# Down projection of a diffusion layer: inner partial sums kept in PSUM, a new order of the seven inner products, and last residual rows written into PSUM ahead of the products

## The chip, the core and the metric

The kernel runs on one core of a Trainium2 chip. The time is the device time of one launch in microseconds (us), the median of several runs. The engines are TensorE (PE, with its weight loads as PEld), VectorE (DVE), ScalarE (ACT), GpSimd (POOL) and SyncE (SP), which issues the transfers here.

## The reference

One layer of a diffusion backbone with 2048 positions and a width of 1024: a token mixer, then a SwiGLU block, each with a residual and a layer norm behind it. The change touches only the last product, `@ wd`, with the sum and the norm around it:

```python
def swiglu(u, wg, wu, wd):
    return (jax.nn.silu(u @ wg) * (u @ wu)) @ wd
...
        u2 = modulate(layer_norm(x), sh2, sc2)
        x = layer_norm(DEEPNORM_ALPHA * x + gt2 * swiglu(u2, w_ffn_gate[l], w_ffn_up[l], w_ffn_down[l]),
                       ln2_g[l], ln2_b[l])
```

The hidden width is 2816, so this product is (2048 x 2816) by (2816 x 1024). The gate `gt2` is multiplied into the weights beforehand.

## The kernel before

All products here are made from two fp16 parts (a high one and the rest), three matmuls for each, by `mm3` (L152 to L154). The down projection takes about the last 437 us (1757 to 2194), and is a Strassen-Winograd scheme of two levels.

**The outer level** has seven operands: A11, A12, S2, S3, A22, S1, S4. The hidden activations (float32 for the first five, `h_d`) and the weights (`wd_d`) of each lie in DRAM, written by earlier stages. The results go into 16 tiles of SBUF named `state`, one for each half `sb` of the rows, each half f of such a half, and each of the names "a", "11", "21" and "22", [128, 2, 512] in float32. A11 begins "a"; A12 plus "a" is "11", which is one quadrant of the output; S2 is added to "a"; S3 plus "a" is "21", which is copied to "22"; A22 is added to "21". S1 and S4 complete "22" and "a".

**The inner level** applies to the first five outer operands. For each o of these and each `sb`, in this text a *step* (A11/0, A11/1, A12/0, and so on, ten in all), the hidden block is cut into four quadrants `h0` to `h3`, loaded by `h_load` into one buffer each in the order 0, 2, 3, 1. `h_ops` makes the seven inner operands out of them. Names A11 to S4 stand for these too; the index into the tuple is the product:

```python
                if i == 1:
                    G.tensor_tensor(s1, q[2], q[3], ALU.add)
                    V.tensor_tensor(q[2], q[0], q[2], ALU.subtract)
                    V.tensor_tensor(q[0], s1, q[0], ALU.subtract)
                elif i == 2:
                    G.tensor_tensor(q[1], q[1], q[0], ALU.subtract)
                t = op((q[0], q[1], q[0], q[2], q[3], s1, q[1])[i])
```

So A11 is `h0` and A12 is `h1`. Then POOL makes `s` (tile `s1`, h2 + h3, L1394), VectorE makes S3 in the place of `h2` (L1395) and S2 in the place of `h0` (L1396), and POOL makes S4 in the place of `h1` (L1398). A22 is `h3` itself and S1 is `s`. Each operand is split into a tile `ho` by `half_split`: ScalarE casts the high part (L1134), VectorE subtracts it for the low part (L1135). There are three buffers of `ho`. The seven products of a step run in the order A11, A12, S2, S3, A22, S1, S4; each has 30 matmuls of [128 x 128] by [128 x 256], and four of them have 6 more ("ride", for the 22nd hidden block, with its own small operand in a tile named `raw`), 234 in all. Each product takes the next one of the eight PSUM banks in turn (`proj`, `misc`, `tq`, `zt`, `s0`, `s1`; the trace prints the last two as `s`, as it does the SBUF tile).

Behind each product, results are read out of its bank: ScalarE copies A11 to an SBUF tile `p` (L1500); VectorE adds A12 to `p` into a tile `c`, S2 onto `p`, S3 to `p` into `b`, A22 to `b` into `c`, S1 onto `p`, and `p` or `b` to a bank into `c` for the rest (L1504 to L1511, and L1443 in `outer`). `outer` then adds `c` to a state (L1445 to L1452), SBUF to SBUF. When a half f of a step is complete, `block_done` adds residual rows for A12 (to "11"), S3 (to "a" and "22") and A22 (to "21"), by one VectorE instruction over 1024 columns each (L1411), with the rows loaded into a `raw` tile (three buffers). For A12 and A22 `moments` follows, with statistics for the norm (L1419).

**The last two outer operands**, S1 and S4 (`ONE`), run without an inner level, as products 512 wide over four banks; `after` adds a bank to its states and ends the norm (`finish`).

The order of instructions on each engine is that of a list scheduler that simulates the program when it is built; the blocks under `tc.high_priority()` go ahead of others. SP's queue issues all loads of these steps in that order; `issue_after(before)` holds the loads of a step behind the last `h` load of the step before. A load of `h` waits until its buffer's last reader in the step before is done. With a step of sb 0, SP also loads the seven weight tiles of that operand (`w_load`, L1207).

Of the kernel before, what the change touches and what calls it, by code (L numbers as in the profile page):

```python
# [11 lines left out]
AF = mybir.ActivationFunctionType  # L12
# [67 lines left out]
def layer_kernel(ctx: ExitStack, tc: tile.TileContext, a, out):  # L80
# [19 lines left out]
    def mk(pool, shape, dt=F32, tag=None, bufs=1):  # L100
        return pool.tile(shape, dt, name=nm(tag), tag=tag, bufs=bufs)
# [26 lines left out]
    def raw_tile(shape=(P, 2, 512), dt=F32):  # L128
        return mk(wp, list(shape), dt, tag="raw", bufs=3)
# [809 lines left out]

    A11, A12, S2, S3, A22, S1, S4 = range(7)  # L940
    ORDER = (A11, A12, S2, S1, S3, A22, S4)

    def left(q, s, eng):

# [425 lines left out]
    def state(name, sb, f):  # L1370

        key = (name, sb, f)
        if key not in ST:
            ST[key] = mk(dq, [P, 2, 512], tag="state", bufs=16)
        return ST[key]

    def h_ops(q, last):

        lt = raw_tile((P, 2, 768), F16)
        with tc.high_priority():  # L1380
            half_split(lt[:, :, 0:512], last)
            G.tensor_tensor(last[:, 0:256], last[:, 0:256], last[:, 256:512], ALU.subtract)
            half_split(lt[:, :, 512:768], last[:, 0:256])

        def op(src):
            t = mk(d1, [P, 2, HP, 256], F16, tag="ho", bufs=3)
            half_split(t, src)
            return t

        s1 = mk(d1, [P, HP, 256], tag="s1")  # L1390
        for i in range(7):
            with tc.high_priority():
                if i == 1:
                    G.tensor_tensor(s1, q[2], q[3], ALU.add)  # L1394
# [5 lines that stand above are left out]
            yield t, lt  # L1400
# [1 line left out]

    RIDE = {1: (0, 0), 4: (1, 0), 5: (1, 1), 6: (2, 1)}

    def residual(sb, f, name, row, hf):
        s_ = state(name, sb, f)
        xr = raw_tile((P, 2, 512))
        for i in range(2):
            t = sb * 8 + row * 4 + f * 2 + i
            Q.dma_start(xr[:, i], x1_d[t][:, hf * 512 : hf * 512 + 512])  # L1410
        V.scalar_tensor_tensor(s_, xr, ALPHA * RS, s_, ALU.mult, ALU.add)  # L1411

    st6 = {}

# [15 lines left out]
            V.tensor_tensor(r, r, b2[:, fs], ALU.add)  # L1430
            Q.dma_start(outv[t * P : (t + 1) * P, fs], r)

    def outer(o, sb, f, y, src, ps):


        def st(name):
            return state(name, sb, f)[:, :, y * 256 : (y + 1) * 256]

        if o == A11:
            V.tensor_tensor(st("a"), src, ps, ALU.add)  # L1440
            return
        c = mk(dq, [P, 2, 256], tag="c", bufs=2)
        V.tensor_tensor(c, src, ps, ALU.add)  # L1443
        if o == A12:
            V.tensor_tensor(st("11"), st("a"), c, ALU.add)  # L1445
        elif o == S2:
            V.tensor_tensor(st("a"), st("a"), c, ALU.add)
        elif o == S3:
            V.tensor_tensor(st("21"), st("a"), c, ALU.add)
            S.copy(st("22"), st("21"))  # L1450
        else:
            V.tensor_tensor(st("21"), st("21"), c, ALU.add)  # L1452

    def block_done(o, sb, f):

        if o == A12:
            residual(sb, f, "11", 0, 0)
            for i in range(2):
                moments(sb, f, i, "11", 0, 0)
        elif o == S3:  # L1460
            residual(sb, f, "a", 0, 1)
            residual(sb, f, "22", 1, 1)
        elif o == A22:
            residual(sb, f, "21", 1, 0)
            for i in range(2):
                moments(sb, f, i, "21", 0, 1)

    for o in range(5):
        for sb in range(2):
            if o == 0 and sb == 0:  # L1470
                w = w_next
                hq, last, before = h_next
                w.update((q, w_load(0, q)) for q in (5, 6))
            else:

                with tc.issue_after(before):
                    if sb == 0:
                        w = {0: w_load(o, 0)}
                    hq, last, before = h_load(o, sb)
                    if sb == 0:  # L1480
                        wl = wl_load(o)
                        w.update((q, w_load(o, q)) for q in range(1, 7))
            if o == 0 and sb == 1:
                g2 = rows(dq, a["ln2_g"], "row0")
                b2 = rows(dq, a["ln2_b"], "row1")
            p = b_ = None
            for q, (h, lt) in enumerate(h_ops(hq, last)):
                ps = bank(ALL_BANKS, (P, 2, 256))
                ride = RIDE.get(q)
                for i in range(2):  # L1490
                    ts_ = slice(i * P, (i + 1) * P)
                    for k in range(HP):
                        mm3(ps[:, i], h[:, 0, k, ts_], h[:, 1, k, ts_], w[q][k][:, :, 0], w[q][k][:, :, 1], k == 0, k == HP - 1 and ride is None)
                    if ride:
                        r0 = ride[0] * 256 + i * P
                        ys = slice(ride[1] * 256, ride[1] * 256 + 256)
                        mm3(ps[:, i], lt[:, 0, r0 : r0 + P], lt[:, 1, r0 : r0 + P], wl[:, 0, ys], wl[:, 1, ys], False, True)
                if q == 0:
                    p = mk(dq, [P, 2, 256], tag="p", bufs=2)
                    S.copy(p, ps)  # L1500
                elif q == 1:
                    outer(o, sb, 0, 0, p, ps)
                elif q == 2:
                    V.tensor_tensor(p, p, ps, ALU.add)  # L1504
                elif q == 3:
                    b_ = mk(dq, [P, 2, 256], tag="b", bufs=1)
                    V.tensor_tensor(b_, p, ps, ALU.add)
                elif q == 4:
                    outer(o, sb, 1, 0, b_, ps)
                elif q == 5:  # L1510
                    V.tensor_tensor(p, p, ps, ALU.add)  # L1511
                    outer(o, sb, 1, 1, b_, ps)
                    block_done(o, sb, 1)
                else:
                    outer(o, sb, 0, 1, p, ps)
                    block_done(o, sb, 0)


    slots = [(tag, 1) for tag in ("h0", "h2", "h3", "s1", "h1")] + [("ho", 3)] * 3
# [28 lines left out]
    for o in ONE:  # L1548
        w = one_w(o)
        for sb in range(2):  # L1550
            h = one_h(o, sb)
            pts = [bank(ALL_BANKS) for _ in range(4)]

            def product(j, it):
                ts_ = slice(it * P, (it + 1) * P)
                mm3(pts[it], h[j][:, 0, ts_], h[j][:, 1, ts_], w[j][:, :, 0], w[j][:, :, 1], j == 0, j == HJ - 1)

            def after(it):
                f, i = divmod(it, 2)
                pv = pts[it].rearrange("p (c y n) -> p y c n", c=2, y=2)  # L1560

                def add(name):
                    r = state(name, sb, f)[:, i].rearrange("p (y c n) -> p y c n", c=2, y=2)
# [50 lines left out]
```

## Time and profile before

| | |
|---|---|
| median of three runs | 2194.33 us (2192.77 to 2195.07) |
| the profiled execution | 2195.93 us, span 2194.1 us |
| TensorE (PE) busy | 2051.6 us, 94% of the span |
| VectorE (DVE) busy | 1487.7 us, 68% |
| GpSimd (POOL) busy | 845.6 us, 39% |
| ScalarE (ACT) busy | 803.5 us, 37% |
| mean granted TensorE clock | 0.973 of full speed |

The shares are means over the whole program; the change concerns 1757 us to the end. TensorE is close to always busy, so what is to be read is where it waits in that part and for what.

### The profile page before, as it was taken

To read this page: it belongs to the slowest core of one execution; us is meant where nothing else is said; L and a number is where in the kernel's file an instruction comes from. 1 tells how busy PE (TensorE), PEld (TensorE's weight loads), DVE (VectorE), ACT (ScalarE), POOL (GpSimd) and SP (SyncE) were. 2 spreads that over 40 slices of the span, in tenths; PEclk is the share of its full clock that TensorE was granted. 3 is DMA by queue.
4 is the path that set the end of the run, shared out by engine and by line. 5 is a ranking of instruction groups with operands and counts; after the bars stand their busy time and mean duration, and the time that the engine had idled before them with its cause. 6 is when DMAs were issued, how large, how long until landed. Compare 5 with 4: busy or idle time off the path is not lost. (4 is left out here: it accounts for less than half of the span.)

```text
span 2194.1 us, 31196 instructions
## 1 busy us (share of the span) xinstructions
PE 2051.6 (94%) x11678; PEld 1185.6 (54%) x11678; DVE 1487.7 (68%) x2731; ACT 803.5 (37%) x1442; POOL 845.6 (39%) x838
## 2 busy tenths in 40 slices
PE   6987999999999999889999999999999979898997
PEld 4545676567558444434444444444443458776743
DVE  7767584765688677876656665666556278878866
ACT  5634542332223244443343333333433233333222
POOL 3412321221221156656556655665565142222110
PEclk8998999999999999989999999999999989999999
DMA  9502321221142566614343334343434186779543
GB/s 285 175 4 77 106 80 49 78 61 47 55 119 90 194 209 218 207 66 154 126 144 133 118 129 150 126 136 130 139 116 156 55 266 189 214 213 278 200 146 128
DMA packets 308745, 305.20 MB, mean 139 GB/s; under 512 B 14753, under 2 KB 248049, under 8 KB 307441
## 3 DMA queue, kind: packets, MB, share of 16 engines
q1 hardware_dynamic: 301776, 287.08, 40.9%
q10 hardware_dynamic: 6816, 16.12, 2.0%
q8 instruction: 92, 1.51, 0.3%
q14 instruction: 61, 0.49, 0.1%
HBM read 200.25 MB, written 102.90 MB: 138 GB/s over the span
## 5 line engine op out<-in xcount | busy, mean ns | idle before, releaser
L152 PE MATMUL proj<-ws,uhi 128*128 128x512 f16 (+1 forms) x768 | 251.1, 327 | 2.1 <-ACT sg L751 1.0
L154 PE MATMUL proj<-ws,ulo 128*128 128x512 f16 (+1 forms) x768 | 250.8, 327 | 0.0
L153 PE MATMUL proj<-ws,uhi 128*128 128x512 f16 (+1 forms) x768 | 250.7, 326 | 0.0
L153 PEld LDWEIGHTS <-ws 128*128 128x128 f16 x1296 | 128.2, 99 | 175.9 <-issue 26.6
L152 PEld LDWEIGHTS <-ws 128*128 128x128 f16 x1296 | 128.4, 99 | 157.1 <-issue 9.4
L154 PEld LDWEIGHTS <-ws 128*128 128x128 f16 x1296 | 128.0, 99 | 156.4 <-issue 6.7
L149 DVE SCALAR_TENSOR_TENSOR ws<-raw,ws 128x512 f16<-128x512 f32 x186 | 156.1, 855 | 75.3 <-ACT ws L148 74.3
L148 ACT ACTIVATE ws<-raw 128x512 f16<-128x512 f32 x186 | 112.4, 624 | 124.3 <-DMA raw<-in_w_ffn_gate_dram 36.6
L152 PE MATMUL proj<-u2b,ws 128*128 128x512 f16 x340 | 128.8, 383 | 10.3 <-ACT b L1294 6.3
L152 PE MATMUL misc<-u2a,ws 128*128 128x512 f16 x344 | 131.6, 382 | 6.0 <-ACT p L1294 3.8
L153 PE MATMUL misc<-u2a,ws 128*128 128x512 f16 x344 | 131.8, 383 | 0.0
L154 PE MATMUL misc<-u2a,ws 128*128 128x512 f16 x344 | 131.7, 383 | 0.0
L154 PE MATMUL proj<-u2b,ws 128*128 128x512 f16 x340 | 130.2, 383 | 0.0
L153 PE MATMUL proj<-u2b,ws 128*128 128x512 f16 x340 | 130.1, 383 | 0.0
L1134 ACT CAST ho<-h 128x1280 f16<-128x1280 f32 x60 | 75.0, 1258 | 126.3 <-DMA h<-h 29.0
L149 DVE SCALAR_TENSOR_TENSOR wdo<-raw,wdo 128x256 f16<-128x256 f32 (+1 forms) x100 | 63.4, 655 | 84.8 <-ACT wdo L148 83.8
L167 POOL TENSOR_TENSOR rstd<-ve,mhalf 128x1 f32<-128x1 f32 x66 | 38.4, 590 | 200.8 <-DVE ve L165 177.9
L207 DVE SCALAR_TENSOR_TENSOR macc<-raw,sil,macc 128x128 f32<-128x128 f32 x308 | 109.2, 387 | 3.2
L1135 DVE TENSOR_TENSOR ho<-h,ho 128x1280 f16<-128x1280 f32 x60 | 104.2, 1743 | 9.7 <-ACT ho L1134 9.7
L149 DVE SCALAR_TENSOR_TENSOR wdo<-ws,wdo 128x512 f16<-128x512 f32 (+2 forms) x70 | 59.3, 868 | 75.8 <-ACT wdo L148 74.3
L154 PEld LDWEIGHTS <-ho 128*128 128x128 f16 x764 | 76.2, 100 | 51.1 <-DVE ho L1135 34.2
L152 PEld LDWEIGHTS <-uhi 128*128 128x128 f16 x768 | 75.8, 99 | 44.0 <-issue 2.5
(496 smaller groups left out, 5498.6 us busy)
## 6 DMA issues: line engine op xcount, KB each, us to landing
h<-h SPq DMA_DIRECT2D x40, 640.0 KB, 5.4
raw<-in_w_mod_dram SPq DMA_DIRECT2D x44, 512.0 KB, 4.1
wd<-wdo SPq DMA_DIRECT2D x50, 448.0 KB, 2.5
wd<-wd SPq DMA_DIRECT2D x33, 640.0 KB, 8.5
h<-sg SPq DMA_DIRECT2D x66, 256.0 KB, 2.6
raw<-in_w_ffn_gate_dram SPq DMA_DIRECT2D x22, 512.0 KB, 4.7
raw<-in_w_ffn_up_dram SPq DMA_DIRECT2D x22, 512.0 KB, 5.8
h<-hs SPq DMA_DIRECT2D x44, 256.0 KB, 2.0
```

The lines of the kernel that those rows point to most:

```text
L148: S.activation(hi, raw, AF.Copy, scale=scale)
L149: V.scalar_tensor_tensor(lo, raw, scale, hi, ALU.mult, ALU.subtract)
L152: T.matmul(o, sh, mh, start=first, stop=False, skip_group_check=onto)
L153: T.matmul(o, sh, ml, start=False, stop=False, skip_group_check=onto)
L154: T.matmul(o, sl, mh, start=False, stop=last, skip_group_check=onto)
L167: pows.append(G.tensor_tensor(rstd, ve, mhalf[:, 0:n], ALU.pow).ins)
L207: V.scalar_tensor_tensor(acc, raw[:, k], sil[:, v, k : k + 1], acc, ALU.mult, ALU.add)
L1134: S.copy(dst[:, 0], src)
L1135: V.tensor_tensor(dst[:, 1], src, dst[:, 0], ALU.subtract)
```

## The change

Each step now lets its products accumulate in PSUM. The order of products is `DOWN`: A11, A12, S2, S1, S3, S4, A22. Three banks serve a step: one (`x`) for A11, S2, S3 and A22 on top of each other, one for A12, and one (`z`) for S1 and S4. Between two products on a bank it is read out: after A11, A12, S2, S1, S3, S4 and A22, the last seen sum goes from the bank to a state at once, in one VectorE instruction by the table `INTO` (for the first A11 of a state a copy by ScalarE). The tiles `p`, `b` and `c` are gone. "22" is no longer copied from "21": its residual instruction reads "21" and writes "22". The residual rows of the states "a" are no longer added in step S3; in the outer S4 stage ScalarE writes them, scaled, into the four banks before the first matmul, and the matmuls accumulate onto them (`onto`).

```diff
+    DOWN = (A11, A12, S2, S1, S3, S4, A22)
...
-        for i in range(7):
+        for i in DOWN:
...
+    def x1_half(t, hf):
+        return x1_d[t][:, hf * 512 : hf * 512 + 512]
+
+    def residual(sb, f, name, row, hf, onto=None):
+
         xr = raw_tile((P, 2, 512))
         for i in range(2):
-            t = sb * 8 + row * 4 + f * 2 + i
-            Q.dma_start(xr[:, i], x1_d[t][:, hf * 512 : hf * 512 + 512])
-        V.scalar_tensor_tensor(s_, xr, ALPHA * RS, s_, ALU.mult, ALU.add)
+            Q.dma_start(xr[:, i], x1_half(sb * 8 + row * 4 + f * 2 + i, hf))
+        V.scalar_tensor_tensor(state(name, sb, f), xr, ALPHA * RS, state(onto or name, sb, f), ALU.mult, ALU.add)
...
-    def outer(o, sb, f, y, src, ps):
-
+
+    INTO = {A11: ("a", None), A12: ("11", "a"), S2: ("a", "a"), S3: ("21", "a"), A22: ("21", "21")}
+    begun = set()
+
+    def outer(o, sb, f, y, ps):
+
+        into, of = INTO[o]
+        if (o, sb, f, y) in begun:
+            of = into
+        begun.add((o, sb, f, y))
...
-        if o == A11:
-            V.tensor_tensor(st("a"), src, ps, ALU.add)
-            return
-        c = mk(dq, [P, 2, 256], tag="c", bufs=2)
-        V.tensor_tensor(c, src, ps, ALU.add)
...
-            V.tensor_tensor(st("21"), st("a"), c, ALU.add)
-            S.copy(st("22"), st("21"))
+        if of is None:
+            S.copy(st(into), ps)
         else:
-            V.tensor_tensor(st("21"), st("21"), c, ALU.add)
+            V.tensor_tensor(st(into), st(of), ps, ALU.add)
...
-            residual(sb, f, "a", 0, 1)
-            residual(sb, f, "22", 1, 1)
+            residual(sb, f, "22", 1, 1, "21")
...
+            x = z = None
+            for q, (h, lt) in zip(DOWN, h_ops(hq, last)):
+                onto = x if q in (S2, S3, A22) else z if q == S4 else None
+                ps = bank(ALL_BANKS, (P, 2, 256)) if onto is None else onto
...
+                        mm3(
+                            ps[:, i], h[:, 0, k, ts_], h[:, 1, k, ts_], w[q][k][:, :, 0], w[q][k][:, :, 1],
+                            onto is None and i == 0 and k == 0, k == HP - 1 and ride is None, skip,
+                        )
...
+                if q == A11:
+                    x = ps
+                    outer(o, sb, 0, 0, x)
+                elif q == A12:
+                    outer(o, sb, 0, 0, ps)
+                elif q == S2:
+                    outer(o, sb, 0, 1, x)
+                elif q == S1:
+                    z = ps
+                    outer(o, sb, 1, 1, z)
+                elif q == S3:
+                    outer(o, sb, 1, 1, x)
+                elif q == S4:
+                    outer(o, sb, 0, 1, z)
+                    block_done(o, sb, 0)
+                else:
+                    outer(o, sb, 1, 0, x)
                     block_done(o, sb, 1)
...
+            onto = o == S4
+            if onto:
+                for it in range(4):
+                    xr = raw_tile((P, 512))
+                    Q.dma_start(xr, x1_half(sb * 8 + it, 1))
+                    S.activation(pvs[it], xr.rearrange("p (y c n) -> p y c n", c=2, y=2), AF.Copy, scale=ALPHA * RS)
```

On ScalarE, these rows are the casts of the seven operands of step A12/0 into `ho`, and what else stands among them; the tile read stands behind the arrow, so `h0` to `h3` are the quadrants and `s1` the sum. Before:

```order
L1134 CAST ho_2864_16814<-h0_2850_16783 128x1280
L1134 CAST ho_2867_16853<-h1_2853_16789 128x1280
L1134 CAST ho_2871_16898<-h0_2850_16783 128x1280
L1134 CAST ho_2873_16933<-h2_2851_16785 128x1280
L1500 COPY p_2866_16848<-tq_2865_16817 128x512
L1134 CAST ho_2876_16969<-h3_2852_16787 128x1280
L1134 CAST ho_2880_17013<-s1_2863_16813 128x1280
L1134 CAST ho_2886_17065<-h1_2853_16789 128x1280
```

Of the change (its lines stand one or a few further down):

```order
L1135 CAST ho_2852_16800<-h0_2838_16769 128x1280
L1135 CAST ho_2855_16839<-h1_2841_16775 128x1280
L1451 COPY state_2833_16651<-s1_2826_16499 128x2x256
L1135 CAST ho_2857_16881<-h0_2838_16769 128x1280
L1135 CAST ho_2858_16915<-s1_2851_16799 128x1280
L1135 CAST ho_2861_16957<-h2_2839_16771 128x1280
L1135 CAST ho_2862_16991<-h1_2841_16775 128x1280
L1135 CAST ho_2866_17039<-h3_2840_16773 128x1280
```

The cast of `h3` moved from fifth of the seven to last, that of the sum from sixth to fourth.

On SP, these rows are the loads of step A12/1 (`h` quadrants, then the block for the small operand, `ws`, and its weights). Before:

```order
L1216 DMA h0_2892_17116<-h_1956_9749 128x5x256
L1216 DMA h2_2893_17118<-h_1956_9749 128x5x256
L1216 DMA h3_2894_17120<-h_1956_9749 128x5x256
L1216 DMA h1_2895_17122<-h_1956_9749 128x5x256
L1218 DMA ws_2932_17445<-h_1944_9743 128x512
L1223 DMA ws_2933_17447<-wl_1986_9764 128x1024
```

Of the change:

```order
L1217 DMA h0_2870_17087<-h_1956_9749 128x5x256
L1217 DMA h2_2871_17089<-h_1956_9749 128x5x256
L1217 DMA h1_2873_17093<-h_1956_9749 128x5x256
L1219 DMA ws_2900_17401<-h_1944_9743 128x512
L1224 DMA ws_2901_17403<-wl_1986_9764 128x1024
L1217 DMA h3_2872_17091<-h_1956_9749 128x5x256
```

The load of `h3` moved from the third place to the last, behind `h1` and the two `ws` tiles.

On VectorE, these rows are the boundary from A12/0 to A12/1: the splits of the new step (`ho` from `h`), the two sums that make its operands (L1395 and L1396 before, L1396 and L1397 now), and what is left of the old step. Before:

```order
L1135 TENSOR_TENSOR ho_2899_17133<-h0_2892_17116,ho_2899_17133 128x1280
L1396 TENSOR_TENSOR h0_2892_17116<-s1_2898_17132,h0_2892_17116 128x1280
L1511 TENSOR_TENSOR p_2866_16848<-p_2866_16848,s1_2881_17016 128x512
L1443 TENSOR_TENSOR c_2882_17054<-b_2875_16967,s1_2881_17016 128x512
L1135 TENSOR_TENSOR ho_2902_17172<-h1_2895_17122,ho_2902_17172 128x1280
L1445 TENSOR_TENSOR state_2879_17011<-state_2817_16397,c_2882_17054 128x2x256
L1443 TENSOR_TENSOR c_2888_17105<-p_2866_16848,proj_2887_17068 128x512
L1411 SCALAR_TENSOR_TENSOR state_2879_17011<-raw_2883_17057,state_2879_17011 128x1024
L1445 TENSOR_TENSOR state_2870_16895<-state_2809_16283,c_2888_17105 128x2x256
L1135 TENSOR_TENSOR ho_2906_17217<-h0_2892_17116,ho_2906_17217 128x1280
```

Of the change:

```order
L1136 TENSOR_TENSOR ho_2880_17143<-h1_2873_17093,ho_2880_17143 128x1280
L1396 TENSOR_TENSOR h2_2871_17089<-h0_2870_17087,h2_2871_17089 128x1280
L1422 BN_STATS st6_2864_17035<-state_2854_16834 128x6
L1422 BN_STATS st6_2865_17037<-state_2854_16834 128x6
L1136 TENSOR_TENSOR raw_2875_17097<-ws_2874_17095,raw_2875_17097 128x512
L1453 TENSOR_TENSOR state_2860_16955<-state_2812_16359,tq_2853_16803 128x2x256
L1397 TENSOR_TENSOR h0_2870_17087<-s1_2876_17103,h0_2870_17087 128x1280
L1453 TENSOR_TENSOR state_2879_17138<-state_2827_16530,misc_2878_17107 128x2x256
L1414 SCALAR_TENSOR_TENSOR state_2860_16955<-raw_2867_17079,state_2860_16955 128x1024
L1136 TENSOR_TENSOR raw_2875_17097<-ws_2874_17095,raw_2875_17097 128x256
L1136 TENSOR_TENSOR ho_2882_17185<-h0_2870_17087,ho_2882_17185 128x1280
```

The two operand sums stand behind the split of A12 and among statistics and a read-out of the old step now; the sum in the place of `h0` (L1396 before, L1397 now) stood ahead of the split of A12 and now stands behind it. No row adds an SBUF tile `c` to a state any more.

## Rows read from the trace of the kernel before

**Rows 1.** Windows: start and end (us), length, busy time (instructions) by engine, clock, DMA.
```profile
core 0: us, PE busy (x) PEld busy (x) DVE busy (x) ACT busy (x) POOL busy (x), PEclk, DMA share, GB/s
1757.00:1831.00 74.00, 60.07 (x484) 49.12 (x483) 58.38 (x46) 24.20 (x27) 29.32 (x12) 0.91 0.89 270
1831.00:1856.50 25.50, 25.50 (x236) 22.78 (x235) 21.18 (x19) 9.29 (x8) 5.80 (x2) 1.00 0.54 171
1856.50:1887.40 30.90, 27.20 (x237) 23.56 (x235) 24.96 (x28) 8.96 (x9) 6.85 (x3) 0.94 0.73 220
1887.40:1918.70 31.30, 26.16 (x237) 22.57 (x235) 31.30 (x32) 12.92 (x14) 8.89 (x4) 1.00 0.54 158
1918.70:1946.40 27.70, 25.88 (x237) 22.72 (x234) 20.93 (x21) 8.28 (x8) 7.24 (x3) 1.00 0.77 223
1946.40:1975.90 29.50, 26.06 (x236) 22.65 (x234) 24.78 (x23) 11.69 (x11) 6.12 (x2) 1.00 0.63 188
1975.90:2007.20 31.30, 27.04 (x236) 23.41 (x234) 28.91 (x26) 11.24 (x13) 7.44 (x3) 0.95 0.81 240
2007.20:2040.80 33.60, 27.75 (x236) 23.32 (x235) 30.07 (x28) 12.29 (x13) 8.74 (x3) 0.95 0.87 283
2040.80:2070.10 29.30, 27.38 (x244) 23.41 (x241) 28.05 (x31) 7.64 (x8) 5.14 (x2) 1.00 0.70 249
2070.10:2127.00 56.90, 56.90 (x267) 25.86 (x265) 26.24 (x53) 5.97 (x8) 2.94 (x4) 1.00 0.47 145
```

**Rows 2.** Waits, 1831 to 2070: group, releaser, idle us, count, longest.
```profile
PEld L154 <- DVE ho L1135: 25.7, 13, 4.5
```

**Rows 3.** Timeline of PE in A12/1: start, duration, wait and releaser in brackets.
```profile
1865.69 0.39 PE L154 MATMUL zt<-wd,ho 128*128 128x256 f16 x1 [3.69 <-DVE ho L1135]
```

**Rows 4.** Timeline of DVE, 1856.9 to 1868.7.
```profile
1859.70 0.68 DVE L1443 TENSOR_TENSOR c<-p,proj 128x512 f32<-128x512 f32 x1
1860.30 3.33 DVE L1411 SCALAR_TENSOR_TENSOR state<-raw,state 128x1024 f32<-128x1024 f32 x1
1864.15 1.48 DVE L1135 TENSOR_TENSOR ho<-h,ho 128x1280 f16<-128x1280 f32 x1
...
1867.35 1.20 DVE L1411 SCALAR_TENSOR_TENSOR state<-raw,state 128x1024 f32<-128x1024 f32 x1
```

**Rows 5.** Timeline of POOL in the same stretch.
```profile
1859.31 3.23 POOL L1398 TENSOR_TENSOR h<-h,h 128x1280 f32<-128x1280 f32 x1 [8.51 <-DVE ho L1135]
```

**Rows 6.** The chain of waits: first at 1840 to 1850, then at 1873 to 1892.
```profile
1842.44 5.30 DMA h<-h
1847.91 2.91 POOL s L1394
...
1875.46 8.28 DMA h<-h
```

**Rows 7.** One window behind the wait of rows 3; columns as in rows 1.
```profile
1865.40:1868.80 3.40, 3.11 (x15) 2.24 (x16) 3.40 (x6) 0.41 (x1) 0.73 (x1) 0.50 0.83 259
```

**Rows 8.** Groups of ScalarE, 1757 to 2195: count, busy, mean ns, idle before.
```profile
L1134 ACT CAST ho<-h 128x1280 f16<-128x1280 f32 x60 | 75.0, 1258 | 126.3 <-DMA h<-h 29.0 <-PE misc L154 23.6 <-PE s L154 21.3
L1500 ACT COPY p<-proj 128x512 f32<-128x512 f32 x3 | 1.7, 578 | 0.0
```

**Rows 9.** DMA issues, 1757 to 2066: count, size, median us to landing.
```profile
h<-h SPq DMA_DIRECT2D x36, 640.0 KB, 4.7
wd<-wd SPq DMA_DIRECT2D x31, 640.0 KB, 8.5
```

**Rows 10.** Groups of VectorE by form, 1757 to 2075; columns as in rows 8.
```profile
L1395 DVE TENSOR_TENSOR h<-h,h 128x1280 f32<-128x1280 f32 x10 | 14.9, 1486 | 20.3 <-POOL s L1394 20.3
L1419 DVE BATCH_NORM_STATS2 st<-state 128x6 f32<-128x512 f32 x16 | 10.2, 678 | 0.1
```

**Rows 11.** Timeline of SP at 1783: a weight load of the first step.
```profile
1782.99 3.66 SPq L1207 DMA_DIRECT2D wd<-wd  x2
```

**Rows 12.** Timeline of PE: last matmul of the fifth product, then of the eighth.
```profile
1789.80 0.27 PE L154 MATMUL proj<-ws,raw 128*128 128x256 f16 x1
...
1808.56 0.27 PE L154 MATMUL zt<-wd,ho 128*128 128x256 f16 x1
```

More of the change, by code (lines that the diff above doesn't have):

```diff
@@ L1403, in layer_kernel @@
     RIDE = {1: (0, 0), 4: (1, 0), 5: (1, 1), 6: (2, 1)}
-    def residual(sb, f, name, row, hf):
-        s_ = state(name, sb, f)
+    def x1_half(t, hf):
+        return x1_d[t][:, hf * 512 : hf * 512 + 512]
+    def residual(sb, f, name, row, hf, onto=None):
         xr = raw_tile((P, 2, 512))
         for i in range(2):
-            t = sb * 8 + row * 4 + f * 2 + i
-            Q.dma_start(xr[:, i], x1_d[t][:, hf * 512 : hf * 512 + 512])
-        V.scalar_tensor_tensor(s_, xr, ALPHA * RS, s_, ALU.mult, ALU.add)
+            Q.dma_start(xr[:, i], x1_half(sb * 8 + row * 4 + f * 2 + i, hf))
+        V.scalar_tensor_tensor(state(name, sb, f), xr, ALPHA * RS, state(onto or name, sb, f), ALU.mult, ALU.add)
     st6 = {}
@@ L1485, in layer_kernel @@
                 b2 = rows(dq, a["ln2_b"], "row1")
-            p = b_ = None
-            for q, (h, lt) in enumerate(h_ops(hq, last)):
-                ps = bank(ALL_BANKS, (P, 2, 256))
+            x = z = None
+            for q, (h, lt) in zip(DOWN, h_ops(hq, last)):
+                onto = x if q in (S2, S3, A22) else z if q == S4 else None
+                ps = bank(ALL_BANKS, (P, 2, 256)) if onto is None else onto
                 ride = RIDE.get(q)
@@ L1491, in layer_kernel @@
                     ts_ = slice(i * P, (i + 1) * P)
+                    skip = onto is not None or i > 0
                     for k in range(HP):
-                        mm3(ps[:, i], h[:, 0, k, ts_], h[:, 1, k, ts_], w[q][k][:, :, 0], w[q][k][:, :, 1], k == 0, k == HP - 1 and ride is None)
+                        mm3(
+                            ps[:, i], h[:, 0, k, ts_], h[:, 1, k, ts_], w[q][k][:, :, 0], w[q][k][:, :, 1],
+                            onto is None and i == 0 and k == 0, k == HP - 1 and ride is None, skip,
+                        )
                     if ride:
@@ L1496, in layer_kernel @@
                         ys = slice(ride[1] * 256, ride[1] * 256 + 256)
[L1497 to L1512, printed above, removed]
+                        mm3(ps[:, i], lt[:, 0, r0 : r0 + P], lt[:, 1, r0 : r0 + P], wl[:, 0, ys], wl[:, 1, ys], False, True, skip)
+                if q == A11:
[15 more added lines that the diff above has]
+                    outer(o, sb, 1, 0, x)
                     block_done(o, sb, 1)
-                else:
-                    outer(o, sb, 0, 1, p, ps)
-                    block_done(o, sb, 0)
     slots = [(tag, 1) for tag in ("h0", "h2", "h3", "s1", "h1")] + [("ho", 3)] * 3
@@ L1552, in layer_kernel @@
             pts = [bank(ALL_BANKS) for _ in range(4)]
+            pvs = [pt.rearrange("p (c y n) -> p y c n", c=2, y=2) for pt in pts]
+            onto = o == S4
[4 more added lines that the diff above has]
+                    S.activation(pvs[it], xr.rearrange("p (y c n) -> p y c n", c=2, y=2), AF.Copy, scale=ALPHA * RS)
             def product(j, it):
                 ts_ = slice(it * P, (it + 1) * P)
-                mm3(pts[it], h[j][:, 0, ts_], h[j][:, 1, ts_], w[j][:, :, 0], w[j][:, :, 1], j == 0, j == HJ - 1)
+                mm3(pts[it], h[j][:, 0, ts_], h[j][:, 1, ts_], w[j][:, :, 0], w[j][:, :, 1], j == 0 and not onto, j == HJ - 1, onto)
             def after(it):
                 f, i = divmod(it, 2)
-                pv = pts[it].rearrange("p (c y n) -> p y c n", c=2, y=2)
+                pv = pvs[it]
                 def add(name):
```

5 lines of the change are left out of this document (removed).

## The prediction, made before the changed kernel ran

> **What bounds the kernel now.** I read the windows first, step by step. A step is one outer operand o on one half sb of the rows: seven products, 234 matmuls. Step A12/0 ran at 25.50 us with TensorE busy throughout [rows 1], so 0.109 us per matmul, 3.3 us for a product of 30 and 3.9 for one of 36, and 25.5 us is what a step costs when nothing is late. The seven steps behind it took 30.9, 31.3, 27.7, 29.5, 31.3, 33.6 and 29.3 us: 35.1 us over. The first two steps took 74.0 us, 23.0 over. In the S1 stage TensorE is busy for all of 56.9 us [rows 1]; nothing is to be had there. So the change acts on some 58 us of lateness, in 313 us.
>
> What ends the waits: TensorE's weight load waits for VectorE's `ho` (the low half of the split operand), 25.7 us in 13 waits [rows 2]. VectorE is busy for 76 to 100% of each late step [rows 1]; where it is late it is not always short of time. At the largest wait of A12/1, 3.69 us [rows 3], the residual ahead of `ho` took 3.33 us [rows 4], where its twin took 1.20, because POOL's update of `h` ran from 1859.31 to 1862.54 [rows 5]: an instruction with two SBUF operands stood still until POOL was done. The sum beside it, with one operand in PSUM, ran in the same POOL instruction at 0.68. The other lateness comes through the chain DMA of `h`, POOL `s` (2.9 us), L1395, L1396, `ho`: the transfer took 5.3 us at one boundary, 8.28 at another that also loads weights [rows 6]. And the clock: after a wait of 3.7 us the granted clock was 0.50 (1.2 GHz) for 3.4 us, with 3.11 us of matmuls in it [rows 7], which costs 1.6 us.
>
> **What the change removes.** Per step VectorE had 11 read-outs (7 in A11's steps), now 7 (3 in A11's): 40 fewer of 0.60 us start to start [rows 4], 24 us. Four residuals (1.2 us) of the states "a" go to ScalarE. So some 29 us leave, of the 269 us that VectorE is busy from 1757.0 to 2070.1 [rows 1]. No instruction of a state has two SBUF operands any more but the residuals. ScalarE loses 18 copies and gains 8 read-outs of A11 and 8 PSUM writes of a like size (0.58 us [rows 8]): nothing. The writes need the banks and the x rows; they lie under the second S1 product (TensorE 56.9 us of 56.9, ScalarE 6.0 [rows 1]). Without that cover they would cost 4 x 0.6 us twice, 5 us. Their 8 DMAs replace 8 of the old residuals. The last products and the tail keep their instructions.
>
> **What it moves.** `DOWN` puts A22 last, and A22 is the only product that reads `h3`. Three `ho` buffers turn, so the split for A22 waits for the product three before it. Before, A22 was fifth and waited for the second product; now it is seventh and waits for the fourth (S1). `h3` comes free 7.2 us later, and the next step's S1, S2 and S4 operands all begin with POOL's h2 + h3. The order lists show it: SP now issues `h3` last, and the split of A22 stands last of seven.
>
> I count from E = the end of S1. The step's last product ends at E+11.1, the next A11 at 14.4, A12 at 18.3; S2's third matmul, which needs `ho`, would run at 18.7. Read-out of S1 0.7, cast of A22 to 1.4 (1.26 [rows 8]), its split to 2.9 (1.48 [rows 4]). Then the load: 4.7 us (median [rows 9]) where the step loads no weights; between 4.7 and 8.28 where it does, I take 7.0, nearer to the row of such a boundary. POOL 2.9; L1395 and L1396 1.49 each [rows 10], with the read-out of A22 between; then POOL's second update (3.2 us) starts, and the next `ho` has two SBUF operands and stands until it ends, then needs 1.4.
> - S2/0 to S2/1 (no weights, no residual): POOL 7.8 to 10.7; `ho` of A12, held, to 12.1; L1395 13.5; read-out 14.1; L1396 15.5; POOL to 18.8; `ho` 20.2. Late by 1.5.
> - S2/1 to S3/0 (weights): POOL 10.1 to 13.0; L1395 14.5; 15.1; L1396 16.5; POOL to 19.8; `ho` 21.2. Late by 2.5. A11/1 to A12/0 has one read-out less: 1.9.
> - A12/0 to A12/1 (residuals and statistics): the first residual held to 11.8, `ho` of A12 13.2, L1395 14.6, two statistics (0.68 [rows 10], 0.6 in a row) 15.8, the split of `raw` (as the 512 sums, 0.6) 16.4, read-out 17.0, L1396 18.4, POOL to 21.7, second residual 22.8, short split 23.2, `ho` 24.6. Late by 5.9, plus 1.6 of clock: 7.5. A22/0 to A22/1 the same.
> - A12/1 to S2/0: the load at 7.0, POOL to 13.0, the same list to 24.2: 5.5 + 1.6. S3/0 to S3/1, without statistics: 22.9, 4.2 + 1.6. S3/1 to A22/0: 23.9, 5.2 + 1.6.
>
> Sum: 1.9 + 7.5 + 7.1 + 1.5 + 2.5 + 5.8 + 6.8 + 7.5 = 40.6, against 35.1: +5.5.
>
> The first two steps: S1 is fourth now and needs weights that SP issued at 1782.99 [rows 11], when S2 ends (the fifth product ended at 1789.8; less the 66 matmuls of two products, 1782.6 [rows 12]). They land after 4.7 to 8.5 us [rows 9], 1787.7 to 1791.5. From there 3.9 + 3.3 + 3.9 + 3.9, 1.6 of clock and A11's 3.3: eight products at 1807.6 to 1811.4, where before it was 1808.56 [rows 12]; +0.9 in the middle, and 0.6 at the boundary behind it. Together with the +5.5 that is +7.0.
>
> The profiled execution took 2195.93 us, 1.6 over the median of the runs; against the median of 2194.33 the sum gives 2201.
>
> **Rivals.**
> *Fewer instructions win.* If the `h3` loop does not decide (the load lands by E+5, or POOL's second update does not hold the next `ho`), the same lists end 3 to 5 us earlier: plain boundaries are not late, those with residuals by 0.6 to 1.5. Lateness falls from 35.1 to some 5, and the time to about 2165; half of it gives 2180. For it: VectorE really loses 29 us, and 13 waits are for it. Against: every two-operand instruction that met POOL in the rows above stood still. The Trainium skill ("VectorE: DVE Perf Modes", Rules for kernel authors) says to minimise the number of VectorE instructions; by that rule 24 us would come back. The rows say that an instruction's neighbour and its place matter more here.
>
> *The bank's readers.* S2, S3 and A22 write into the bank that was read out after A11, S2 and S3, so TensorE now waits for read-outs that once had eight banks of slack. One product of 3.3 us covers a read-out of 0.7; it decides where a read-out starts more than 2.6 us after its product. The held residual lost 2.1 us [rows 4], and a read-out behind such a one and a split would be 1 to 2 us too late. Once a step, on ten steps, over the sum: 2201 + 10 = 2211. Against: the lists put the read-out ahead of the split that is late anyway. The skill ("PSUM — Partial Sum Buffer", Summary) advises to read PSUM from a bank other than the one being written, guarded by bank; no row of before shows what the guard costs.
>
> *The load is slow.* With 8.28 us at all nine boundaries the plain ones are late by 3.7 and the others by 8 to 9 with the clock: 2218.
>
> *No difference.* If the load takes 4.7 us at the weight boundaries too, some 5 us leave the sum, and it is 2196.
>
> **How the numbers follow.** 0.2%, 4.4 us, is about what a measurement of this kernel can tell from no change. The loop as summed, spread 7 us: chance 0.55, of which about 0.37 lies above 2198.7, 0.15 within 0.2% (with the no-difference case in it) and 0.03 below. Fewer instructions win: 0.22. Bank readers: 0.10. Slow load: 0.08. The rest 0.05, which I put down as no difference but for 0.01 slower. Faster: 0.22 + 0.03 = 0.25. Same: 0.15 + 0.04 = 0.19. Slower: 0.37 + 0.10 + 0.08 + 0.01 = 0.56. The range: 2182 leaves 0.12 out below (the full gain), 2214 some 0.08 above. The likeliest case alone: 2192 to 2210.
>
> **What would show it.** Right: between 1831 and 2070 VectorE busy some 24 us less, but TensorE idle as before or more, in one place per step, at S2's third matmul, released by `ho`; POOL `s` starting 8 us and more after S1's end; `ho` of S2 with 2 to 3 us instead of 1.48, inside POOL's update; read-outs of states never held. The first step: S1 waiting for a DMA of `wd` at about 1783 to 1790. Wrong: steps of 25.5 to 27 us with residuals in them; waits of TensorE ahead of S3, S4 or A22, released by a read-out; POOL's `s` ending before A22 ends.

## The result, and the profile after

The changed kernel took 2215.07 us (median of four runs, 2211.35 to 2218.04) against 2194.7 us of before in the same runs: ratio 1.0092, interval 1.0075 to 1.011 (95%). It is 20 us slower, clear of the noise. Slower was forecast, but by 7 us, and the range ended at 2214.

The page of the profiled execution (2215.17 us):

```profile
span 2213.4 us, 31155 instructions
...
PE 2061.2 (93%) x11678; PEld 1190.0 (54%) x11678; DVE 1465.1 (66%) x2687; ACT 803.0 (36%) x1440; POOL 841.6 (38%) x838
```

VectorE has 44 instructions and 23 us of busy time less, and the span is 19.3 us longer. The windows say where. They are cut at the first matmul of a step; the first holds both A11 steps, the last is the S1 stage (columns as in [rows 1]):

```profile
1758.20:1835.40 77.20, 61.80 (x480) 49.93 (x481) 51.93 (x40) 26.77 (x31) 27.27 (x12) 0.89 0.87 264
1835.40:1863.60 28.20, 25.87 (x237) 22.67 (x235) 20.15 (x15) 9.20 (x8) 8.59 (x3) 1.00 0.42 135
1863.60:1896.80 33.20, 28.25 (x236) 23.72 (x234) 27.84 (x27) 10.25 (x10) 4.07 (x3) 0.90 0.72 215
1896.80:1930.80 34.00, 28.46 (x237) 23.76 (x235) 29.26 (x27) 10.96 (x12) 11.62 (x6) 0.90 0.47 135
1930.80:1958.00 27.20, 25.67 (x236) 22.73 (x234) 20.62 (x17) 8.61 (x7) 3.05 (x2) 1.00 0.82 238
1958.00:1989.20 31.20, 27.71 (x236) 23.49 (x235) 20.62 (x17) 9.23 (x8) 8.43 (x3) 0.95 0.57 168
1989.20:2020.90 31.70, 27.24 (x237) 23.38 (x235) 26.34 (x22) 9.64 (x9) 5.62 (x3) 0.95 0.76 240
2020.90:2056.50 35.60, 29.30 (x236) 23.99 (x235) 23.03 (x20) 9.22 (x9) 9.37 (x4) 0.86 0.66 204
2056.50:2089.00 32.50, 28.38 (x240) 23.79 (x238) 25.25 (x25) 6.92 (x7) 3.63 (x2) 0.95 0.68 223
2089.00:2145.90 56.90, 56.90 (x267) 25.92 (x265) 23.72 (x48) 8.98 (x13) 2.93 (x4) 1.00 0.57 178
```

The S1 stage is 56.9 us of busy TensorE, as in [rows 1]. Nearly everything lies in the ten steps. The eight from A12/0 on took 253.5 us; in [rows 1] they took 239.1. VectorE is busy less in their sum (not in each: A12/1 has 27.84 us, before 24.96), and none of the eight runs at 25.5 us any more. The waits of TensorE's weight load, 1835 to 2089:

```profile
PEld L154 <- DVE ho L1136: 17.8, 8, 3.2
PEld L152 <- ACT ho L1135: 17.7, 12, 4.8
```

Before it was 25.7 us for `ho` from VectorE [rows 2]. Now a second group as large waits for ScalarE's cast: S2's operand is late as a whole, so its first matmul waits for the high part, and its third again for the low one. One boundary, S3/1 to A22/0, as the chain of waits has it:

```profile
2014.69 1.22 DVE ho L1136
2015.91 8.18 DMA h<-h
2024.28 2.87 POOL s L1395
2027.17 2.00 DVE h L1396
2029.17 0.60 DVE state L1453
2029.83 0.20 issue
2030.03 1.49 DVE h L1397
2031.62 1.27 ACT ho L1135
2032.91 3.00 DVE ho L1136
2035.95 0.39 PE proj L154
```

It is the predicted loop link by link: load, POOL's sum, two operand sums, cast, split, matmul. The split takes 3.00 us, where 1.48 is usual [rows 4], since POOL's second update begins at 2031.65:

```profile
2024.25 2.89 POOL L1395 TENSOR_TENSOR s<-h,h 128x1280 f32<-128x1280 f32 x1 [24.47 <-DMA h<-h]
...
2031.65 2.89 POOL L1399 TENSOR_TENSOR h<-h,h 128x1280 f32<-128x1280 f32 x1 [3.83 <-DVE h L1397]
```

The chain puts the load down to the split just ahead of it, but that one is the next step's A11. The split of A22, on which the `h3` buffer waits, had its cast at 2009.80, at the end of S1, and was done at 2012.6. SP's timeline has what came between:

```profile
2010.87 4.95 SPq L1543 DMA_DIRECT2D ws<-wd  x5
2015.91 1.18 SPq L1217 DMA_DIRECT2D h<-h  x1
```

Five weight loads of the S1 stage stood ahead of the `h3` load in SP's queue. The prediction has no such term.

### The profile page after: what moved, and what is told of

It is laid out like the page before. It is cut to its first block, busy times and chain, and to the rows that moved or that the text cites. A ratio compares the mean times of both kernels' runs of the same rounds, so it can differ in the third digit from the quotient of the medians.

```text
span 2213.4 us, 31155 instructions
## 1 busy us (share of the span) xinstructions
PE 2061.2 (93%) x11678; PEld 1190.0 (54%) x11678; DVE 1465.1 (66%) x2687; ACT 803.0 (36%) x1440; POOL 841.6 (38%) x838
## 3 DMA queue, kind: packets, MB, share of 16 engines
q1 hardware_dynamic: 301776, 287.08, 40.6%
## 5 line engine op out<-in xcount | busy, mean ns | idle before, releaser
L149 DVE SCALAR_TENSOR_TENSOR wdo<-ws,wdo 128x512 f16<-128x512 f32 (+2 forms) x70 | 59.6, 870 | 74.8 <-ACT wdo L148 73.3
```

The source lines that it names most:

```text
L149: V.scalar_tensor_tensor(lo, raw, scale, hi, ALU.mult, ALU.subtract)
```

## Experiments

Ratios are to the kernel before, timed on the same chip beside each group of runs. The lengths of the ten steps, from the first matmul of each to that of the next, read from the one trace of each run (the two A11 steps stand first, and the tenth step is counted to its last matmul):

```
before              48.0 25.5 | 25.5 30.9 31.3 27.7 29.5 31.3 33.7 29.2
changed             50.1 27.1 | 28.2 33.2 34.0 27.2 31.2 31.7 35.6 32.4
e1_a22_last         44.2 35.3 | 26.0 29.9 37.6 30.3 30.0 33.4 36.3 34.4
e2_h3_two           47.4 25.9 | 25.5 27.5 28.2 27.1 25.5 27.5 30.1 27.4
e3_a22_third        43.8 25.5 | 26.3 27.5 35.0 25.5 28.8 30.4 30.7 27.4
e4_presets_only     47.0 25.5 | 25.5 30.5 30.6 27.5 28.6 28.5 31.5 32.1
e5_no_weights       50.5 27.1 | 26.9 34.1 34.2 26.7 25.8 31.4 33.3 33.7
e6_h1_on_dve        48.1 25.9 | 27.6 31.4 33.0 25.9 29.8 30.7 33.9 33.9
e7_last_first       49.0 25.8 | 25.5 27.3 28.4 28.8 25.5 27.4 28.8 27.4
e8_w5_early         44.7 25.9 | 25.5 27.6 28.2 28.2 25.5 27.5 30.3 27.4
e9_after_w5         44.7 33.6 | 26.7 34.0 34.2 26.8 31.2 32.0 36.0 32.3
e10_before_h3_two   42.1 26.0 | 25.5 27.2 30.3 27.1 25.5 29.5 31.5 31.0
e11_s1w_held        49.3 27.1 | 28.6 33.3 33.9 26.7 31.2 33.5 32.0 33.5
e12_best_a          44.0 25.9 | 25.5 26.1 31.5 25.5 25.5 26.4 26.6 32.1
```

The start of the first step lies between 1755.8 and 1761.3 us in these traces, whatever the kernel; so much of a span is not the down projection's. The tenth step also holds the matmuls of the S1 stage that ran within it, 0.22 us each: 7 before, 3 in the changed kernel, 12 in e10, 10 in e4 and e6, 3 or fewer in the others.

**e1_a22_last.** The kernel before, with A22 moved from fifth to last.

```diff
-        for i in range(7):
+        for i in (A11, A12, S2, S3, S1, S4, A22):
...
-            for q, (h, lt) in enumerate(h_ops(hq, last)):
+            for q, (h, lt) in zip((A11, A12, S2, S3, S1, S4, A22), h_ops(hq, last)):
```

> The kernel before with nothing changed but that A22 is the last of the seven products (A11, A12, S2, S3, S1, S4, A22); p, b and c stay in SBUF, and so do all 40 read-outs. Theory (the loop over h3: its buffer comes free later, so its load, POOL's sum and the next step's S2 operand are late): as slow as the changed kernel or slower, 2205 to 2225 us, with waits of 2 to 8 us at S2 of nearly every step. Rival (products on top of each other in a bank cost the time, by waits for read-outs): within 5 us of before, 2190 to 2200.

2226.38 us, ratio 1.0137 (1.0117 to 1.0157). The place of A22 alone costs 30 us, with all read-outs kept (the residual rows that wait for A22 move behind it). In the traces 19 us of it lie in the eight steps and 6 in the first two; 3.5 are a later start of the first step. The weight load of TensorE waits 15.9 us for casts and 13.6 us for splits of `ho`, as in the changed kernel, and 14.6 us for the split of the small block, which the changed kernel does not have in its list. The rest of the change then gives back some 10 us (1.0137 less 1.0092, of 2194), though S1's place differs between the two.

**e2_h3_two.** The changed kernel with a second buffer for `h3`.

```diff
-            r[qd] = mk(d1, [P, HP, 256], tag=f"h{qd}")
+            r[qd] = mk(dq if qd == 3 and sb else d1, [P, HP, 256], tag=f"h{qd}")
```

> The changed kernel with a second buffer for h3 (steps of the second half of the rows use their own), so that the load of h3 no longer waits for the split of A22. Order and read-outs stay. Theory (h3 loop): POOL's sum starts 6 us and more earlier in every step, the waits at S2 fall from 50 us over eight steps to under 15, and the time to 2165 to 2185, faster than before. Rival (bank read-outs, or VectorE and POOL holding each other whatever the load does): POOL starts earlier, but the step lengths stay within 1 us of those of the changed kernel, 2205 to 2217.

2180.26 us, ratio 0.9926 (0.9909 to 0.9942): 36 us less than the changed kernel by the ratios, and faster than before. The eight steps fell from 253.5 to 218.8 us, so from 49.5 us late to 14.8. POOL's sum now starts between 0.5 us before and 3.8 us after the end of S1; at A22/0, where the changed kernel had 14.4 us, it starts 2.0 us after it:

```profile
1986.56 3.40 POOL L1395 TENSOR_TENSOR s<-h,h 128x1280 f32<-128x1280 f32 x1 [10.51 <-DMA h<-h]
```

Its waits, 1831 to 2095:

```profile
PEld L154 <- DVE raw L1136: 9.0, 5, 3.0
PEld L153 <- issue: 4.8, 7, 1.7
```

The wait for `ho` is gone from the list, and one for the split of the small block took a part of its place. Banks, read-outs and the order of products are those of the changed kernel; what differs is when the load may start, and what the scheduler makes of it. So the loop over `h3` is what the changed kernel loses its time by; how much of that the kernel before lost too, e10 shows.

**e3_a22_third.** A22 third, in a bank of its own, with eight read-outs a step.

```diff
-    DOWN = (A11, A12, S2, S1, S3, S4, A22)
+    DOWN = (A11, A12, A22, S2, S1, S3, S4)
...
-                onto = x if q in (S2, S3, A22) else z if q == S4 else None
+                onto = x if q in (S2, S3) else z if q == S4 else None
```

> The changed kernel with the order A11, A12, A22, S2, S1, S3, S4; A22 has a bank of its own, and the third sum in bank x is read out into two states, so 8 read-outs a step in place of 7. Theory (h3 loop): h3 comes free with the third product, S2 comes 3.9 us later in the step, so both ends of the loop get slack: waits under 10 us over eight steps, 2160 to 2180. Rival (bank read-outs): one more of them, so no better than the changed kernel, 2205 to 2220.

2184.02 us, ratio 0.9948 (0.9931 to 0.9965): the direction of the theory, without a new buffer, but 4 us short of its range. S2/0 still took 35.0 us, and 22.6 us of waits for `ho` are left. The longest of TensorE's, 4.97 us, ended at 1893.00, with a split beside which POOL's update ran from 1888.71 to 1891.59:

```profile
1889.00 3.94 DVE L1136 TENSOR_TENSOR ho<-h,ho 128x1280 f16<-128x1280 f32 x1
```

**e4_presets_only.** The kernel before, with the PSUM rows of the S4 stage in place of the four residuals of "a".

```diff
-            residual(sb, f, "a", 0, 1)
...
+                    S.activation(pvs[it], xr.rearrange("p (y c n) -> p y c n", c=2, y=2), AF.Copy, scale=ALPHA * RS)
```

> The kernel before with the last part of the change alone: the four residuals of the states a are gone from step S3, and in the S4 stage ScalarE writes the scaled rows into the four banks before the matmuls. Theory: the part is harmless; 5 us of VectorE's work leave the two S3 steps, whose boundaries were 5.8 and 8.1 us late, so 2 to 6 us are won, 2188 to 2193. Rival: the writes into the banks hold up the S4 stage by 2 to 5 us, 2195 to 2200.

2192.68 us, ratio 0.9984 (0.9972 to 0.9996). It wins 3.5 us, as expected, and its two S3 steps are 3.7 us shorter. The interval only just leaves 1 out.

**e5_no_weights.** The changed kernel without most weight loads of the later operands.

```diff
-                        w.update((q, w_load(o, q)) for q in range(1, 7))
+                        w.update((q, w_load(o, q)) for q in (3, 4) if o == 1)
```

> The changed kernel without 22 of the weight loads of the second to fifth outer operand (products 1 to 6, but for 3 and 4 of the second); these products use the weights that lie in the buffers from before, so this part of the result is another. What it sizes: at the boundaries into S2/0, S3/0 and A22/0 the loads of h3 share their time, or SP's queue, with weight loads. Theory (that share is what the prediction had too small): these three boundaries, 8.5, 5.7 and 10.1 us late, come down to 6, 2 and 7, so some 9 us are won, 2203 to 2209. Rival (POOL and VectorE holding each other is all that counts): within 3 us of the changed kernel, 2212 to 2218.

The kernel leaves out loads that its result needs; only its time is read. 2208.57 us, ratio 1.0062 (1.0046 to 1.0078), 6.6 us less than the changed kernel: near the theory in sum, not in its places. From the issue of the `h3` load to POOL's sum it is 4.8, 4.0 and 4.1 us into A12/0, S2/0 and S3/0, where the changed kernel has 8.3, 7.1 and 9.2; into A22/0, whose loads of the S1 stage stayed, 9.0. S3/0 fell by 5.4 us, to 25.8, and A12/0 by 1.3, but S2/0 not at all. There the earlier sum only met the residual: `ho` came 24.6 us after the end of S1, with the weight loads 24.9. At a boundary with residuals and statistics the load is not what ends last; VectorE's list and POOL's update are.

**e6_h1_on_dve.** POOL's second update moved to VectorE.

```diff
-                    G.tensor_tensor(q[1], q[1], q[0], ALU.subtract)
+                    pass
...
+            if i == 2:
+                V.tensor_tensor(q[1], q[1], q[0], ALU.subtract)
```

> The changed kernel with POOL's second update of a step (h1 less S2's operand) moved to VectorE, 10 instructions of 1.49 us. Theory (POOL's 2.9 us hold the split of S2, or the residual ahead of it): the split ends some 1.3 us earlier at the eight boundaries, in spite of 15 us more work on VectorE, and the clock falls less; 2202 to 2209. Rival (VectorE is short of time, the hold is an appearance): 10 us slower than the changed kernel, 2220 to 2230.

2205.46 us, ratio 1.0039 (1.0027 to 1.0051): 11.6 us less than the changed kernel, with 15 us more work on VectorE. The waits for the low part of `ho` are down to this, 1831 to 2095:

```profile
PEld L154 <- DVE ho L1136: 12.0, 8, 2.3
```

The wait for the cast stayed at 17.2 us. VectorE's busy time in the eight steps even fell, from 193.1 to 187.9 us. So POOL's update does hold VectorE on the path, and taking away what holds VectorE was worth more here than an instruction fewer on it.

**e7_last_first.** e2 with the small block loaded ahead of the quadrants.

```diff
+        last = ws_tile((P, 512), F32)
+        Q.dma_start(last, h_d[sb][o][:, HJ - 1])
         for qd in (0, 2, 3, 1):
```

> The kernel with two h3 buffers, and the small block of a step (the 22nd hidden block) is loaded ahead of the four quadrants in place of behind them. There the longest waits left in the late steps were for the split of that block, 9.0 us in five. Theory: they go, 2172 to 2177. Rival: that split stands late in VectorE's order whatever the load does, 2178 to 2182.

2180.39 us, ratio 0.9928 (0.9916 to 0.9941), the same as e2. The waits are the same too, so its load was never the reason; the rival holds, that the split stands late in VectorE's order:

```profile
PEld L154 <- DVE raw L1136: 8.9, 5, 3.0
```

**e8_w5_early.** e7 with the first operand's weights of S1 loaded before those of A22.

```diff
-        if o == 0 and q in (3, 4):
+        if o == 0 and q in (3, S1):
...
-                        w_next.update((q, w_load(0, q)) for q in range(1, 5))
+                        w_next.update((q, w_load(0, q)) for q in (1, 2, S1, 3))
...
-                w.update((q, w_load(0, q)) for q in (5, 6))
+                w.update((q, w_load(0, q)) for q in (S4, A22))
```

> The run with two h3 buffers and the small block first, and besides the weights of S1 and A22 of the first outer operand change places in the loading order, so that those of S1, now the fourth product, are there before those of A22, the last. Theory (the first step's wait of 3.6 us at S1 is for its weights): 2 to 4 us less than the run without it. Rival: another wait takes its place, within 1 us of the run without it.

2177.03 us, ratio 0.9909 (0.9895 to 0.9923), 3.4 us less than e7 by the medians, though the two intervals overlap. The first step fell from 49.0 to 44.7 us.

**e9_after_w5.** The same edit on the changed kernel alone.

> The changed kernel with one thing else: the weights of S1 and A22 of the first outer operand change places in the loading order. It sizes the first step's term (predicted +0.9, measured +2 to 3). Theory (S1, now fourth, waits 4 us for its weights): 2 to 4 us less than the changed kernel, ratio to before 1.0075 to 1.0085. Rival (another wait takes its place): ratio 1.009.

2215.51 us, ratio 1.0093 (1.0078 to 1.0108): nothing, so the theory of this run fell. The first step did fall by 5.4 us, to 44.7, and the second rose by 6.5, to 33.6. In the changed kernel the wait for the weights ended at 1790.74:

```profile
1790.74 0.39 PE L152 MATMUL s<-wd,ho 128*128 128x256 f16 x1 [3.78 <-DMA wd<-wd]
```

But POOL's sum for the second step began at 1806.04 there, and with the weights early no earlier:

```profile
1806.91 2.88 POOL L1395 TENSOR_TENSOR s<-h,h 128x1280 f32<-128x1280 f32 x1 [3.30 <-DMA h<-h]
```

The load of `h3` was issued at 1799.93 in the changed kernel, 6.1 us ahead of that sum; in e9 at 1796.96, right behind two weight loads, and it took 9.9 us. S2's third matmul of the second step ran at 1817.56 in the one and at 1817.28 in the other. The wait at S1 was real, and not the one that ended last.

**e10_before_h3_two.** The kernel before, with the second `h3` buffer of e2 and nothing else.

> The kernel before with two h3 buffers and nothing else: with the load of h3 out of the way, what are the 40 read-outs worth? Against the changed kernel with two buffers (ratio 0.9926). Theory (the loop over h3 set part of the 35 us of before too, VectorE's own work the rest): 2183 to 2192, ratio 0.995 to 0.999, so the read-outs are worth 5 to 14 us where the load is not in the way. Rival one (read-outs worth nothing): ratio 0.9926 as well. Rival two (before was not held by h3 at all): ratio 1.000.

2176.71 us, ratio 0.9912 (0.9895 to 0.9928). That is below the theory's range: before was held by `h3` as well, and with the load out of the way the kernel with all 40 read-outs is no slower than the one without (0.9926; the intervals overlap, so by the times the read-outs are worth nothing that can be measured, as rival one had it). By the steps, e10 took 227.6 us for the last eight, e2 218.8; what follows the steps was 2.6 us shorter in e10, some matmuls of the S1 stage having run within the steps. So read-outs, residuals and the new order together are worth 6 us there, in these two traces. The first two steps took 68.1 us in e10 and 73.3 in e2, where S1 is fourth and waits for its weights: 5 us the other way.

Not all of e10's gain is the loop's. Its eight steps are 12.6 us shorter than before's (less the matmuls of the S1 stage), and the first step 5.9, where something else differs: in before POOL's sum for the second step ran into a split of VectorE, which took 4.00 us and kept TensorE waiting. In e10 that sum ran later, and the split took 1.49. Before:

```profile
1790.84 2.88 POOL L1394 TENSOR_TENSOR s<-h,h 128x1280 f32<-128x1280 f32 x1
1791.07 4.00 DVE L1135 TENSOR_TENSOR ho<-h,ho 128x1280 f16<-128x1280 f32 x1 [0.28 <-ACT ho L1134]
1795.13 0.39 PE L154 MATMUL zt<-wd,ho 128*128 128x256 f16 x1 [3.64 <-DVE ho L1135]
```

Taken the same way, the second buffer takes 34.0 us from the eight steps of the changed kernel (e2). So the loop cost the change 21 us more there than it cost before, the rest of the change gave 6 back, and 15 is what those steps became longer.

**e11_s1w_held.** The changed kernel with the weight loads of the S1 stage held behind the last `h3` load.

```diff
-        w = one_w(o)
+        with tc.issue_after(h3_ins[-1]):
+            w = one_w(o)
```

> The changed kernel with the ten weight loads of the S1 stage held on SP's queue until the last h3 load has been issued. In the changed kernel five of them stood ahead of the h3 load of A22/0, which was issued 6.1 us after S1's end in place of 2.8 us. Theory (the queue is a term the prediction left out at that boundary): the h3 load is issued 3 us earlier, A22/0 is 2 to 4 us shorter, ratio 1.0075 to 1.0085. Rival (the load then just takes longer): ratio 1.009.

2215.01 us, ratio 1.0088 (1.0073 to 1.0103): the queue is what made A22/0 long, by 3.6 us (35.6 to 32.0; the load was issued 2.7 us after the end of S1), but S3/1 and A22/1 were 1.8 and 1.1 us longer in this trace, and the times do not tell the two kernels apart. For the whole time it stays open.

**e12_best_a.** The changed kernel with two `h3` buffers, the weights of e8 and the update of e6.

> Two h3 buffers, S1's weights early, and POOL's second update on VectorE, on top of the changed kernel. Theory (what is left at the boundaries with residuals is partly VectorE held by POOL): 2170 to 2176, ratio 0.988 to 0.9905. Rival (there VectorE is now simply the bound, and 15 us more work hurt it): 2178 to 2186, ratio 0.992 to 0.996.

2173.0 us, ratio 0.9899 (0.9885 to 0.9914): the fastest of all, 22 us below before, as the theory said, though its interval overlaps those of e8 and e10.

## Why the prediction was right in its direction and wrong in its size

*The mechanism held.* A22 last frees `h3` late, the load starts late, and S2's operand is late at every boundary. e1 and e2 show it from both sides: put A22 last and lose 30 us; give `h3` a second buffer and win 36. What was named as signs is there: POOL's sum starts 7.7 to 14.4 us after the end of S1 at seven boundaries (6.8 at A22/1; 8 and more had been named), the split of S2 takes about 3 us inside POOL's update at four boundaries, in three others POOL holds the residual ahead of it, and at S3/1 the short split ahead of it (3.11 us, where 0.41 is usual). TensorE's waits are at the first matmuls of S2, too, not only at the third.

*What failed is the size of terms of the sum.* Boundary by boundary, late over 25.5 us, predicted and measured: 1.9 and 2.7 (A12/0), 7.5 and 7.7, 7.1 and 8.5 (S2/0), 1.5 and 1.7, 2.5 and 5.7 (S3/0), 5.8 and 6.2, 6.8 and 10.1 (A22/0), 7.5 and 6.9 (0.6 of it matmuls of the S1 stage). The sum is 49.5, not 40.6. Nearly all of the 9 us lies in the four that load weights, and three terms were too small:

- "Between 4.7 and 8.28 where it does, I take 7.0": from issue to POOL's sum it was 8.3, 7.1, 9.2 and 8.3 us. At S3/0, with no residual behind it, `ho` came 22.8 us after the end of S1 in place of 21.2.
- SP's queue: 3.3 us at A22/0, where the list of loads ahead of `h3` was not read as far as the S1 stage. `ho` came after 26.1 us, not 23.9.
- The clock: 1.6 us at each of five boundaries, by one stretch of 3.4 us at a granted clock of 0.50 [rows 7]. Now such stretches were 6.8 us (A12/1, S2/0) and 10.2 us (A22/0), and S3/0 has one of 3.4 where none was counted. At A22/0 the 28 matmuls behind the wait took 5.91 us instead of 28 x 0.109 = 3.05: 2.9 us. The stretches of A12/1 and A22/0 (columns as in [rows 1]):

```profile
1874.60:1881.40 6.80, 4.60 (x22) 3.32 (x23) 6.73 (x8) 0.00 (x0) 0.00 (x0) 0.50 0.69 215
2031.60:2041.80 10.20, 7.07 (x32) 4.33 (x33) 6.30 (x4) 3.58 (x3) 2.89 (x1) 0.50 0.70 240
```

*The first two steps* were +3.7 us (77.2 against 73.5), not +1.5. The wait for S1's weights was as described, 4 us, but e9 shows that its price was a wrong account: POOL's sum for the second step set the end, and it came no earlier, since its load of `h3` then stood behind two weight loads and took 9.9 us. With 14.4 us in the eight steps, 0.9 by which the first step started later, 0.9 more in the two last stages and 0.6 less behind the last matmul, that is the 19.3 us of the span.

*The rivals.* "Fewer instructions win" was right about its condition and half right about its gain: with the loop out of the way (e2) the kernel is some 15 us faster than before, not 30. But e10 shows that most of this isn't the instructions' doing: without the loop before is as fast. "The bank's readers" hardly came. In the eight steps the one long wait for a read-out was at S2 of S3/1, and the `ho` that S2's third matmul needs came 1.4 us behind it; in the first step S2 waited 2.08 us for ScalarE's read-out of its bank:

```profile
2000.72 0.28 PE L152 MATMUL misc<-wd,ho 128*128 128x256 f16 x1 [3.98 <-DVE state L1453]
1781.86 0.27 PE L152 MATMUL proj<-wd,ho 128*128 128x256 f16 x1 [2.08 <-ACT state L1451]
```

"The load is slow", 2218 us, came nearest to the time; its loads of 8.28 us were met at the boundaries with weights, not at the others (4.0 to 5.6).

*The parts costed at nothing* were right: the PSUM rows lie under a busy TensorE (105.8 us of the 105.8 from 2089.2 to 2195), and e4 gains 3.5 us with them. VectorE's busy time fell by 17 us in the eight steps (the sums of its column, 193.1 us here and 210.2 in [rows 1]), not by some 24: the read-outs left, but the residuals were held longer, 2.1 us a piece in the mean, where before had 1.7 and the undisturbed one of [rows 4] has 1.2 (the lines by form, VectorE; the first before, 1757 to 2075, the others changed, 1758 to 2095):

```profile
L1411 DVE SCALAR_TENSOR_TENSOR state<-raw,state 128x1024 f32<-128x1024 f32 x16 | 26.4, 1660 | 0.1
...
L1414 DVE SCALAR_TENSOR_TENSOR state<-raw,state 128x1024 f32<-128x1024 f32 x12 | 25.4, 2113 | 0.3
...
L1453 DVE TENSOR_TENSOR state<-state,s 128x512 f32<-128x512 f32 x16 | 10.9, 683 | 9.9 <-PE s L154 9.9
```

The read-outs beside them, with one operand in PSUM, stayed at 0.68 us throughout. One reading of before was off, without weight for the sum: its last window [rows 1] holds 244 matmuls, seven of them of the S1 stage, 1.5 us that are work and not lateness.

## What to carry to other kernels

When a change puts steps in another order, follow each input buffer to its last reader and ask when the next load into it can start, and then what else stands in that queue: here the place of one product cost 30 us, and one more buffer of 5 KB a partition won 36 in the changed kernel. Before counting removed instructions as gain, make the cheap run that takes the suspected wait away from both kernels; it showed that the old kernel lost some 13 us of its eight steps to the same loop. And a wait seen in a trace is worth nothing if another chain ends at the same place (e9).

## What the runs showed of the hardware

A VectorE instruction with two SBUF operands and a POOL instruction, which reads SBUF too, held each other up where they met in these rows of the changed kernel, in both directions: the residual took 3.59 us at 1905.24 with POOL's update from 1904.86, and 1.23 at 1893.92 without; POOL's sum took 3.79 us in place of 2.89 at 1986.55, behind VectorE.

```profile
1893.92 1.23 DVE L1414 SCALAR_TENSOR_TENSOR state<-raw,state 128x1024 f32<-128x1024 f32 x1
1905.24 3.59 DVE L1414 SCALAR_TENSOR_TENSOR state<-raw,state 128x1024 f32<-128x1024 f32 x1
1904.86 2.89 POOL L1399 TENSOR_TENSOR h<-h,h 128x1280 f32<-128x1280 f32 x1 [1.48 <-issue]
...
1986.37 1.22 DVE L1414 SCALAR_TENSOR_TENSOR state<-raw,state 128x1024 f32<-128x1024 f32 x1
1986.55 3.79 POOL L1395 TENSOR_TENSOR s<-h,h 128x1280 f32<-128x1280 f32 x1 [18.16 <-DVE state L1453]
```

The Trainium skill ("SBUF — State Buffer", Who interferes with whom) says that a VectorE instruction with two SBUF inputs contends with a GpSimd instruction that reads SBUF, while one with at most one SBUF input does not, outside the performance modes that use two ports. The traces agree: of the 62 read-outs of the steps, each with one operand in PSUM, none took more than 0.689 us (the lines of L1453, shortest, median and longest). What surprised me is the price on the path: moving ten POOL instructions to VectorE won 11.6 us (e6), more than the 24 us of read-outs that the change removed were worth (6 us, with the load out of the way).
